# A two-layer gated decoder trunk on one core: output product in turns, later rope and attention, one more pair of banks

## The chip, the cores and the metric

One Trainium2 chip, one of its cores. The metric is device microseconds for one execution of the whole program, lower is better. The kernel before has a median of 1640.81 us over three runs (1640.46 to 1642.13).

## The reference, cut to what matters

Everything is float32. There are 256 tokens of width 1024, and two layers. Each layer adds five results to the residual stream `x` in turn:

```
x = x + 0.5 * swiglu(rms_norm(x, ffn1_norm), ffn1_w_gu, ffn1_w_down)
h = rms_norm(x, mix_norm);  z = h @ w_in            # q, k, v, HGRN inputs, gates
y_a = dilated_attention(rope(q), rope(k), v) @ w_att_branch   # 4 heads, 3 dilations each
y_b = (rms_norm(hgrn2(...)) * silu(og)) @ w_hgrn_branch       # 8 heads
x = x + (sigmoid(gate_a) * y_a + sigmoid(gate_b) * y_b) @ w_mix_out
x = x + cross_attention(rms_norm(x, xattn_norm), rms_norm(mem, mem_norm), ...)  # 4 heads
x = x + 0.5 * swiglu(rms_norm(x, ffn2_norm), ffn2_w_gu, ffn2_w_down)
```

The result is a last `rms_norm(x, final_norm)`.

## The kernel before

Activations lie with features on the 128 partitions and the 256 tokens along the free axis. A product is computed in blocks of 128x128 weights. Each float32 operand is split in a high and a low part, and three partial products are kept. For one block TensorE runs two matmuls in `fm`: the high weights against both parts of the activation at once (L323, 512 columns) and the low weights against the high part (L324, 256 columns).

**The weight stream.** Weights arrive from memory in the order of use, 16 blocks a transfer, issued by SyncE. `Stream.prep` splits them in *halves* of 8 blocks: ScalarE casts the high parts (tile `whi`, L104), VectorE subtracts for the low parts (tile `wlo`, L110). When the first block of half i is taken, `take` emits the high cast of half i+3 and the low subtraction of half i+2, and then calls `tick`. So the order of the instructions on each engine is the order in which this Python program emits them, and a low part that is emitted behind other VectorE work waits for that work.

**Ticks.** Each tick (one per half) runs the functions whose count set by `defer(n, ...)` has come down to zero, and then one step of one side generator (`side(generator, period)`). Rope, attention, the HGRN recurrence and the norm of the memory are such side work; they stand between the halves of the large products.

**Accumulators.** The large products accumulate in `pair` tiles: two PSUM banks each, a pool of three. Small products use `bank` tiles: one PSUM bank each, a pool of two. An fm product of two output blocks fills one pair in 16 weight blocks (two halves). `fm_beside` fills two pairs, block by block in turns, and hands over both at the end; before the change only the first FFN of the first layer uses it (L336, L337). `add_halves` copies one half of a pair (L344, ScalarE) and adds the other one tick later (L347, VectorE), which frees the pair.

**Places that the change and the prediction speak of.**

- *Memory norm.* `mem_stats` runs as side work in the first FFN of the first layer. `Norm.steps` sums with TensorE (L395), computes the reciprocal root with VectorE and GpSimd (L398, L401), scales an identity matrix (L404) and, two steps later, spreads the result with a matmul (L408).
- *Rope and attention.* `query_key` has an evacuation, `stage1` (L878 to L880: ScalarE copies and a GpSimd product), then one tick later `stage2` (L884, L885 on VectorE), and one tick after that, for the last of a head's three dilations, `attention` begins as side work with period 2. Attention's first step does the scores (L739 in a bank, L743 in a pair) and emits the softmax (L748 to L754); its second step normalises (L756 to L758), an empty step follows, then come the transposes (L765 to L770) and the value product (L777, L779).
- *HGRN.* `hgrn` holds a pair from its output matmuls (L692, L694) until L705, some four ticks later, once for each half of the heads.
- *Mixer output.* After the merged branch products (att and hgrn, whose last results are put in operand form by L277 and L280), `mm_resid` forms `w_mix_out` in four fm products of two blocks each. Each hands its pair to `Resid.take`: two additions into x (L434), then for two blocks of x the next operand (L287 on ScalarE, L288 on VectorE) and the squares for the next norm (L374 on ScalarE, L376 on VectorE).
- *Cross attention.* After the last value product (L988, L989 take it out) four heads form their output in one bank each (L293 to L295), and `o.put` takes each out (L277, L280).
- *The end.* `Last.finish` sums the squares over the partitions: L477 on what was accumulated so far, L478 on the last block's squares (L454).

Of the kernel before, what the change touches and what calls it, by code (L numbers as in the profile page):

```python
# [127 lines left out]
def build(tc, a, nchunks):  # L128
# [25 lines left out]
    def bank():  # L154
        return psum1.tile([P, 512], F32, name="bank")
# [15 lines left out]
    def defer(n, fn):  # L171
        deferred.append([n, fn])
# [193 lines left out]
    class Norm:  # L366
# [25 lines left out]
        def steps(self, keep=None):  # L392
            st = bank()
            for i in range(2):
                nc.tensor.matmul(st[:, i:i + 1], self.acc[:, i * P:(i + 1) * P], ones[:, :1],  # L395
                                 start=True, stop=True)
            ms = tiny.tile([P, 2], F32, name="ms")
            nc.vector.tensor_scalar(ms, st[:, :2], 1.0 / D, EPS, op0=OP.mult, op1=OP.add)  # L398
            pool = tiny if keep is None else consts
            self.r = pool.tile([P, 2], F32, name="rstd" + (keep or ""))  # L400
            nc.gpsimd.tensor_tensor(self.r, ms, mhalf[:, :2], op=OP.pow)  # L401
            dg = tmp()
            for i in range(2):
                nc.vector.tensor_scalar(dg[:, i * P:(i + 1) * P], ident, self.r[:, i:i + 1], None, op0=OP.mult)  # L404
            yield
            yield
            b = bank()
            nc.tensor.matmul(b[:, :T], ones, dg, start=True, stop=True)  # L408
            self.bc = (tiny if keep is None else consts).tile([P, T], F32, name="bc" + (keep or ""))
            nc.scalar.copy(self.bc, b[:, :T])  # L410
# [29 lines left out]
    class Last:  # L440
# [32 lines left out]
        def finish(self, g):  # L473
            st = pair()
            for i in range(2):
                s = slice(i * P, (i + 1) * P)
                nc.tensor.matmul(st[:, i:i + 1], self.acc[:, s], ones[:, :1], start=True, stop=False)  # L477
                nc.tensor.matmul(st[:, i:i + 1], self.sq[:, s], ones[:, :1], start=False, stop=True)  # L478
            ms = tiny.tile([P, 2], F32, name="ms")
            r = tiny.tile([P, 2], F32, name="rstd")  # L480
            nc.vector.tensor_scalar(ms, st[:, :2], 1.0 / D, EPS, op0=OP.mult, op1=OP.add)
            nc.gpsimd.tensor_tensor(r, ms, mhalf[:, :2], op=OP.pow)
            self.turn(KD - 1, g)
            for i in range(2):
                o, y = self.o[i], a["y"][i * P:(i + 1) * P]
                nc.vector.tensor_scalar(o[:, :512], o[:, :512], r[:, i:i + 1], None, op0=OP.mult)
                nc.scalar.activation(o[:, 512:], self.b[i], AF.Copy, scale=r[:, i:i + 1])
                nc.sync.dma_start(y[:, :512], o[:, :512])
                (nc.sync, nc.scalar)[i].dma_start(y[:, 512:], o[:, 512:])

    def mm_resid(name, l, act, K, res):
        n = 2 if K == KD else 1
        for j in range(0, KD, n):
            fm([(name, l, (j + i) * P, act, K) for i in range(n)],
               lambda left, right, j=j: res.take(j, left, right))

# [238 lines left out]
    def attention(l, h, qk, v, out):  # L735
        b0, b1 = bank(), pair()
        for g in range(NG):
            q, k = qk[g]
            nc.tensor.matmul(b0[:, g * P:(g + 1) * P], q[:, :P], k[:, :P], start=True, stop=True)  # L739
        for g in range(NG):  # L740
            q, k = qk[g]
            d = b1[:, g * T:(g + 1) * T]
            nc.tensor.matmul(d, q[:, P:], k, start=True, stop=True)  # L743
        s0, s1 = slot(), slot()
        sc = float(P) ** -0.5
        mx = tiny.tile([P, 2], F32, name="mx")
        den = tiny.tile([P, 2], F32, name="den")
        nc.vector.scalar_tensor_tensor(s0[:, :384], b0[:, :384], sc, cst[:, C_M0:C_M0 + 384], op0=OP.mult, op1=OP.add)  # L748
        nc.vector.scalar_tensor_tensor(s1[:, :768], b1[:, :768], sc, cst[:, C_M1:C_M1 + 768], op0=OP.mult, op1=OP.add)
        nc.vector.tensor_reduce(mx[:, 0:1], s0[:, :384], axis=AX.X, op=OP.max)  # L750
        nc.vector.tensor_reduce(mx[:, 1:2], s1[:, :768], axis=AX.X, op=OP.max)
        nc.vector.tensor_scalar(mx, mx, -1.0, None, op0=OP.mult)
        nc.scalar.activation(s0[:, :384], s0[:, :384], AF.Exp, bias=mx[:, 0:1], accum_out=den[:, 0:1])
        nc.scalar.activation(s1[:, :768], s1[:, :768], AF.Exp, bias=mx[:, 1:2], accum_out=den[:, 1:2])  # L754
        yield
        nc.vector.reciprocal(den, den)  # L756
        nc.vector.tensor_scalar(s0[:, :384], s0[:, :384], den[:, 0:1], None, op0=OP.mult)
        nc.vector.tensor_scalar(s1[:, :768], s1[:, :768], den[:, 1:2], None, op0=OP.mult)  # L758
        yield
        yield  # L760
        b0, b1 = bank(), pair()
        p0, p1 = slot(), slot()
        for g in range(NG):
            d = b1[:, g * T:(g + 1) * T]
            nc.tensor.transpose(d[:, :P], s0[:, g * P:(g + 1) * P], ident)  # L765
            nc.tensor.transpose(d[:, P:], s1[:, g * T:g * T + P], ident)
        for g in range(NG):
            nc.tensor.transpose(b0[:, g * P:(g + 1) * P], s1[:, g * T + P:(g + 1) * T], ident)
        nc.scalar.copy(p0[:, :768], b1[:, :768])
        nc.scalar.copy(p1[:, :384], b0[:, :384])  # L770
        yield
        while ("v", l) not in flags:
            yield True
        b = bank()
        hs = slice(h * P, (h + 1) * P)
        for g in range(NG):
            nc.tensor.matmul(b[:, :T], v(g, 0)[:, hs], p0[:, g * T:(g + 1) * T], start=g == 0, stop=False)  # L777
        for g in range(NG):
            nc.tensor.matmul(b[:, P:T], v(g, 1)[:, hs], p1[:, g * P:(g + 1) * P], start=False, stop=g == NG - 1)  # L779
        out.put(h, b[:, :T])  # L780
        yield
# [8 lines left out]
    def mixer(l, res, nxt):  # L790
# [76 lines left out]
        def query_key(u):  # L867
# [5 lines left out]
            def evac(left, right):  # L873
# [3 lines left out]
                def stage1():  # L877
                    nc.scalar.copy(r[:64], d[64:])  # L878
                    nc.scalar.copy(r[64:], d[:64])  # L879
                    nc.gpsimd.tensor_tensor(r, r, both(sb), op=OP.mult)  # L880
                    defer(1, stage2)

                def stage2():
                    nc.vector.tensor_tensor(d, d, both(cb), op=OP.mult)  # L884
                    nc.vector.tensor_tensor(d, d, r, op=OP.add)  # L885
                    if g == NG - 1:
                        qk = [(row(2 * i), row(2 * i + 1)) for i in range(NG)]
                        defer(1, lambda: side(attention(l, hd, qk, v, aout), 2))
                add_halves(d, left, right, stage1)
            c = g * 512 + hd * P  # L890
            fm([("w_in", l, CQ + c, h, KD), ("w_in", l, CK + c, h, KD)], evac)
# [29 lines left out]
                add_halves(two(t), left, right, stage1, last)  # L921
            fm([("w_att_branch", l, j * P, aout, AH), ("w_hgrn_branch", l, j * P, hout, HH)], evac)
        r = nxt()
        mm_resid("w_mix_out", l, mg, KD, r)
        return r


# [33 lines left out]
    def xattn(l, res, hm, nxt):  # L961
# [30 lines left out]
        drain()  # L992
        o = Act()
        for hd in range(XH):
            b = bank()
            for d in range(2):
                o0 = (2 * (hd % 2) + d) * P
                for c in range(2):
# [114 lines left out]
```

## Time and profile before

| | |
|---|---|
| median of three runs | 1640.81 us |
| the profiled execution's own time | 1640.77 us |
| its span in the profile | 1639.0 us |
| TensorE busy | 1618.5 us, 99% of the span |
| VectorE busy | 1240.8 us, 76% |
| ScalarE busy | 925.7 us, 56% |
| DMA | mean 176 GB/s |
| granted TensorE clock, mean | 0.998 |

The span runs from the program's first instruction to its last; the profiled execution took 1.8 us more than it. Times in the views are counted from the start of the span. PE is TensorE, PEld its weight loads, DVE VectorE, ACT ScalarE, POOL GpSimd, SP SyncE. Since two matmuls overlap, the end of a matmul in the trace is a model; the distance between the starts of matmuls is the safer measure.

### The profile page before, as it was taken

The numbers are of one execution on the slowest core, as the hardware profiler recorded it, in microseconds if no ns is written. First come the engines' busy times: TensorE is split into PE (matmuls) and PEld (weight loads), VectorE is DVE, ScalarE is ACT, GpSimd is POOL, SyncE is SP. The second block draws the span as 40 slices with busy tenths as digits, with TensorE's granted clock in tenths as the row PEclk, the third lists the DMA queues.
The fourth block names the chain that finished last, engine by engine and source line by source line (L and its number), as shares of the span: only waits on it lengthen the run. The fifth ranks groups of instructions, "written<-read, shape, count | busy, mean of one in ns | idle before, by whom it ended". The sixth has DMA issues, their size and how long they took to land.

```text
span 1639.0 us, 26419 instructions
## 1 busy us (share of the span) xinstructions
PE 1618.5 (99%) x10818; PEld 1414.8 (86%) x10818; DVE 1240.8 (76%) x1804; ACT 925.7 (56%) x1381; POOL 63.0 (4%) x46
## 2 busy tenths in 40 slices
PE   9999999999999999999999999999999999999998
PEld 7888888888888888888888888888888888888887
DVE  7887687767868868877677776777788787688764
ACT  6665454656565656655456655546565656466542
POOL 0000000102100000000000000001111000000000
PEclk9999999999999999999999999999999999999999
DMA  8555554434445534555555564544334454355552
GB/s 303 183 181 211 199 182 180 155 130 154 154 154 180 197 137 171 190 190 196 184 185 197 182 223 176 191 172 150 144 133 159 174 180 179 129 206 180 193 191 79
DMA packets 41593, 288.94 MB, mean 176 GB/s; under 512 B 4864, under 2 KB 4992, under 8 KB 7424
## 3 DMA queue, kind: packets, MB, share of 16 engines
q1 hardware_dynamic: 41040, 286.67, 49.0%
q8 instruction: 85, 1.39, 0.3%
q10 hardware_dynamic: 432, 0.59, 0.1%
q14 instruction: 36, 0.29, 0.1%
HBM read 286.18 MB, written 1.05 MB: 175 GB/s over the span
## 4 chain that ended last, share of the span: by engine, by line
PE 90%; DVE 6%; ACT 2%; issue 1%; DMA 0%; POOLq 0%; POOL 0%; ACTq 0%; DVEq 0%
PE pair L323 49%; PE pair L324 25%; PE pair L297 3%; PE pair L298 3%; PE pair L299 3%; DVE wlo L110 2%; PE bank L645 1%; DVE join L347 1%; DVE slot L280 1%; PE bank L777 1%; PE pair L336 1%; DVE join L917 1%; PE pair L743 0%; PE bank L293 0%; PE bank L294 0%
## 5 line engine op out<-in xcount | busy, mean ns | idle before, releaser
L323 PE MATMUL pair<-slot,whi 128*128 128x512 f32 x3808 | 1337.4, 395 | 4.8 <-DVE slot L280 2.5
L324 PE MATMUL pair<-slot,wlo 128*128 128x256 f32 x3808 | 1065.9, 280 | 0.0
L323 PEld LDWEIGHTS pair<-slot,whi 128*128 128x128 f32 x3808 | 713.4, 187 | 167.4 <-DVE slot L347 3.1
L324 PEld LDWEIGHTS pair<-slot,wlo 128*128 128x128 f32 x3808 | 719.2, 189 | 0.6
L110 DVE TENSOR_TENSOR wlo<-raw,whi 128x1024 fp32r<-128x1024 f32 x532 | 640.1, 1221 | 43.2 <-ACT whi L104 42.9
L104 ACT CAST whi<-raw 128x1024 fp32r<-128x1024 f32 x532 | 546.7, 1046 | 15.5 <-PE pair L299 6.1
L344 ACT COPY join<-pair 128x512 f32<-128x512 f32 x136 | 79.6, 586 | 181.8 <-PE pair L324 181.7
L347 DVE TENSOR_TENSOR join<-pair,join 128x512 f32<-128x512 f32 x136 | 93.7, 690 | 107.1 <-ACT join L344 107.0
L287 ACT ACTIVATE slot<-x,vecs 128x256 fp32r<-128x256 f32 x64 | 30.9, 506 | 133.2 <-DVE x L434 132.0
L297 PE MATMUL pair<-whi,slot 128*128 128x512 f32 x224 | 89.2, 398 | 0.0
L299 PE MATMUL pair<-whi,slot 128*128 128x512 f32 x224 | 87.4, 390 | 0.0
L298 PE MATMUL pair<-wlo,slot 128*128 128x512 f32 x224 | 87.4, 390 | 0.0
L344 ACT COPY slot<-pair 128x512 f32<-128x512 f32 x48 | 28.1, 586 | 102.7 <-PE pair L324 102.7
L277 ACT CAST slot<-join 128x256 fp32r<-128x256 f32 (+1 forms) x120 | 51.7, 435 | 50.8 <-DVE join L919 26.0
L434 DVE SCALAR_TENSOR_TENSOR x<-pair,x 128x256 f32<-128x256 f32 (+1 forms) x80 | 42.5, 531 | 49.2 <-PE pair L324 47.7
L511 ACT ACTIVATE tmp<-join 128x256 f32<-128x256 f32 x88 | 36.4, 417 | 52.5 <-DVE join L510 52.4
L510 DVE TENSOR_TENSOR join<-join,bc 128x512 f32<-128x512 f32 x88 | 60.5, 692 | 5.1 <-ACT bc L410 2.4
L880 POOL TENSOR_TENSOR join<-join,sinb 128x512 f32<-128x512 f32 x24 | 42.1, 1753 | 421.7 <-ACT join L879 392.8
L280 DVE TENSOR_TENSOR slot<-join,slot 128x256 fp32r<-128x256 f32 (+1 forms) x120 | 54.0, 455 | 2.8 <-ACT slot L277 2.8
L347 DVE TENSOR_TENSOR slot<-pair,slot 128x512 f32<-128x512 f32 x48 | 33.1, 689 | 27.5 <-ACT slot L344 27.4
L288 DVE SCALAR_TENSOR_TENSOR slot<-x,vecs,slot 128x256 fp32r<-128x256 f32 x64 | 29.6, 484 | 27.0 <-ACT slot L287 27.0
L299 PEld LDWEIGHTS pair<-whi,slot 128*128 128x128 f32 x224 | 42.0, 188 | 9.0
(184 smaller groups left out, 1029.9 us busy)
## 6 DMA issues: line engine op xcount, KB each, us to landing
raw<-w SPq DMA_DIRECT2D x266, 1024.0 KB, 4.8
slot<-mem SPq DMA_DIRECT2D x6, 512.0 KB, 6.7
raw<-w SPq DMA_DIRECT2D x3, 512.0 KB, 7.8
y<-slot SPq DMA_DIRECT2D x3, 256.0 KB, 2.3
cst<-cst SPq DMA_DIRECT2D x1, 721.0 KB, 10.2
x<-x SPq DMA_DIRECT2D x2, 256.0 KB, 4.3
x<-x SPq DMA_DIRECT2D x1, 512.0 KB, 7.0
raw<-w ACTq DMA_DIRECT2D x1, 256.0 KB, 5.1
```

What stands on the lines that cost most here:

```text
L104: nc.scalar.copy(self.hi[i], r)
L110: nc.vector.tensor_tensor(self.lo[i], r, self.hi[i].bitcast(F32), op=OP.subtract)
L277: nc.scalar.copy(h, src)
L280: nc.vector.tensor_tensor(l, src, h.bitcast(F32), op=OP.subtract)
L297: nc.tensor.matmul(out, ah, wh, start=first, stop=False)
L298: nc.tensor.matmul(out, ah, wl, start=False, stop=False)
L299: nc.tensor.matmul(out, al, wh, start=False, stop=last)
L323: nc.tensor.matmul(whole[:, i * 512:(i + 1) * 512], wh, act.parts(k), start=k == 0, stop=False)
L324: nc.tensor.matmul(whole[:, i * 512:i * 512 + T], wl, act.hi(k), start=False, stop=k == K - 1)
L344: nc.scalar.copy(d, right)
L347: nc.vector.tensor_tensor(d, left, d, op=OP.add)
L510: nc.vector.tensor_tensor(two(t), two(t), both(n.bc), op=OP.mult)
```

## The change

Six edits, which together move work but add or drop no arithmetic:

1. `Norm.steps(keep=...)`, the norm of the memory, yields once more before its last matmul.
2. `Last.finish` issues both sums over the earlier squares, then both over the last ones, and each token block's sum gets a bank of its own.
3. `mm_resid` can form its first four output blocks with `fm_beside`, two pairs by turns; the mixer's output product does so.
4. `stage2` of rope comes two ticks after `stage1` instead of one, and attention starts two ticks after the last `stage2` instead of one.
5. Attention loses the empty step between the normalisation and the transposes.
6. In cross attention the output of heads 2 and 3 goes to half a pair each in place of a bank.

```diff
@@ Norm.steps
             yield
             yield
+            if keep:
+                yield
             b = bank()
@@ Last.finish
             for i in range(2):
-                s = slice(i * P, (i + 1) * P)
-                nc.tensor.matmul(st[:, i:i + 1], self.acc[:, s], ones[:, :1], start=True, stop=False)
-                nc.tensor.matmul(st[:, i:i + 1], self.sq[:, s], ones[:, :1], start=False, stop=True)
+                nc.tensor.matmul(st[:, i * 512:i * 512 + 1], self.acc[:, i * P:(i + 1) * P], ones[:, :1],
+                                 start=True, stop=False)
+            for i in range(2):
+                nc.tensor.matmul(st[:, i * 512:i * 512 + 1], self.sq[:, i * P:(i + 1) * P], ones[:, :1],
+                                 start=False, stop=True)
...
-            nc.vector.tensor_scalar(ms, st[:, :2], 1.0 / D, EPS, op0=OP.mult, op1=OP.add)
+            nc.vector.tensor_scalar(ms, two(st)[:, :, 0], 1.0 / D, EPS, op0=OP.mult, op1=OP.add)
@@ mm_resid
-    def mm_resid(name, l, act, K, res):
+    def mm_resid(name, l, act, K, res, turns=False):
         n = 2 if K == KD else 1
-        for j in range(0, KD, n):
+        first = 0
+        if turns:
+            first = 4
+            fm_beside([(name, l, j * P, act, K) for j in range(4)],
+                      [lambda left, right, j=j: res.take(j, left, right) for j in (0, 2)])
+        for j in range(first, KD, n):
@@ attention, between the normalisation and the transposes
         yield
-        yield
@@ query_key
-                    defer(1, stage2)
+                    defer(2, stage2)
...
-                        defer(1, lambda: side(attention(l, hd, qk, v, aout), 2))
+                        defer(2, lambda: side(attention(l, hd, qk, v, aout), 2))
@@ mixer
-        mm_resid("w_mix_out", l, mg, KD, r)
+        mm_resid("w_mix_out", l, mg, KD, r, True)
@@ xattn
-            b = bank()
+            b = bank() if hd < 2 else pair()[:, :512]
```

In the lists below line numbers of the changed kernel are 2 to 9 higher than before; the names of the tiles tell which instruction is which.

**The mixer's output product, VectorE, from the last operand of the branch products on.** L110 are low parts of weight halves, L434 (before) and L436 (changed) open an evacuation of `Resid.take`, L288 and L376 belong to it. Before:

```order
L280 TENSOR_TENSOR slot<-join,slot 128x256
L110 TENSOR_TENSOR wlo<-raw,whi 128x1024
L280 TENSOR_TENSOR slot<-join,slot 128x256
L110 TENSOR_TENSOR wlo<-raw,whi 128x1024
L434 SCALAR_TENSOR_TENSOR x<-pair,x 128x512 x2
L288 SCALAR_TENSOR_TENSOR slot<-x,vecs,slot 128x256 x2
L376 TENSOR_TENSOR tmp<-tmp 128x256
L110 TENSOR_TENSOR wlo<-raw,whi 128x1024 x2
L434 SCALAR_TENSOR_TENSOR x<-pair,x 128x512 x2
L288 SCALAR_TENSOR_TENSOR slot<-x,vecs,slot 128x256 x2
L376 TENSOR_TENSOR tmp<-tmp 128x256 x2
L110 TENSOR_TENSOR wlo<-raw,whi 128x1024 x2
```

With the change:

```order
L280 TENSOR_TENSOR slot<-join,slot 128x256
L110 TENSOR_TENSOR wlo<-raw,whi 128x1024
L280 TENSOR_TENSOR slot<-join,slot 128x256
L110 TENSOR_TENSOR wlo<-raw,whi 128x1024 x3
L436 SCALAR_TENSOR_TENSOR x<-pair,x 128x512 x2
L288 SCALAR_TENSOR_TENSOR slot<-x,vecs,slot 128x256 x2
L376 TENSOR_TENSOR tmp<-tmp 128x256
L436 SCALAR_TENSOR_TENSOR x<-pair,x 128x512 x2
L288 SCALAR_TENSOR_TENSOR slot<-x,vecs,slot 128x256 x2
L376 TENSOR_TENSOR tmp<-tmp 128x256 x2
L110 TENSOR_TENSOR wlo<-raw,whi 128x1024 x2
```

The two low parts that stood between the first two evacuations now stand ahead of both, and the first two evacuations stand back to back ahead of the next low part.

**The third attention head and the second HGRN output, VectorE.** L748 to L752 take the head's scores, L705 (before) and L714 (changed) read the pair that HGRN holds, L347 frees the pair of a large product. Before:

```order
L347 TENSOR_TENSOR slot<-pair,slot 128x512
L854 TENSOR_TENSOR slot<-slot,bc 128x512
L748 SCALAR_TENSOR_TENSOR slot<-bank,cst 128x384
L749 SCALAR_TENSOR_TENSOR slot<-pair,cst 128x768
L750 TENSOR_REDUCE mx<-slot 128x1
L751 TENSOR_REDUCE mx<-slot 128x1
L752 TENSOR_SCALAR mx<-mx 128x2
L110 TENSOR_TENSOR wlo<-raw,whi 128x1024 x2
L347 TENSOR_TENSOR slot<-pair,slot 128x512
L705 TENSOR_TENSOR slot<-pair,rs 128x512 x2
```

With the change (there L757 to L761 are the head's scores):

```order
L347 TENSOR_TENSOR slot<-pair,slot 128x512
L714 TENSOR_TENSOR slot<-pair,rs 128x512 x2
L110 TENSOR_TENSOR wlo<-raw,whi 128x1024
L757 SCALAR_TENSOR_TENSOR slot<-bank,cst 128x384
L758 SCALAR_TENSOR_TENSOR slot<-pair,cst 128x768
L759 TENSOR_REDUCE mx<-slot 128x1
L760 TENSOR_REDUCE mx<-slot 128x1
L761 TENSOR_SCALAR mx<-mx 128x2
```

The head's scores are now taken after HGRN's pair has been read, where before they were taken while HGRN still held it.

## Rows read from the trace of the kernel before

**Rows 1.** The page's first part (busy time) and its chain, by engine.
```profile
PE 1618.5 (99%) x10818; PEld 1414.8 (86%) x10818; DVE 1240.8 (76%) x1804; ACT 925.7 (56%) x1381; POOL 63.0 (4%) x46
...
PE 90%; DVE 6%; ACT 2%; issue 1%; DMA 0%; POOLq 0%; POOL 0%; ACTq 0%; DVEq 0%
```

**Rows 2.** The waits: who for whom, us in total, times, longest.
```profile
PE pair L323 <- DVE slot L280: 2.5, 2, 1.6
...
PE pair L323 <- DVE slot L347: 2.3, 2, 1.2
...
PE bank L293 <- DVE slot L280: 1.6, 2, 0.8
...
PE bank L739 <- DVE slot L885: 1.5, 2, 0.8
...
PE pair L478 <- ACT tmp L454: 1.3, 1, 1.3
...
PE bank L408 <- DVE tmp L404: 1.0, 1, 1.0
```

**Rows 3.** Timeline of PE, second layer, mixer output: start, us, what, [idle before].
```profile
1319.73 0.27 PE L324 MATMUL pair<-slot,wlo 128*128 128x256 f32 x1
1321.61 0.47 PE L323 MATMUL pair<-slot,whi 128*128 128x512 f32 x1 [1.61 <-DVE slot L280]
```

**Rows 4.** Timeline of PE, first layer, scores of the third head.
```profile
406.45 1.46 PE L743 MATMUL pair<-slot 128*128 128x256 f32 x6
409.08 0.50 PE L323 MATMUL pair<-slot,whi 128*128 128x512 f32 x1 [1.17 <-DVE slot L347]
```

**Rows 5.** Timeline of DVE at the same place, and HGRN's last read there.
```profile
408.34 0.69 DVE L347 TENSOR_TENSOR slot<-pair,slot 128x512 f32<-128x512 f32 x1
...
416.99 1.28 DVE L705 TENSOR_TENSOR slot<-pair,rs 128x512 f32<-128x512 f32 x2
```

**Rows 6.** Timeline of DVE, first layer, rope of the first head.
```profile
304.29 0.69 DVE L885 TENSOR_TENSOR slot<-slot,join 128x512 f32<-128x512 f32 x1
```

**Rows 7.** Timeline of DVE, cross attention, last value evacuation.
```profile
609.18 0.75 DVE L989 SCALAR_TENSOR_TENSOR slot<-pair,rstdmem,slot 128x512 fp32r<-128x512 f32 x1 [0.76 <-ACT slot L988]
```

**Rows 8.** Timeline of PE at the end.
```profile
1631.87 0.36 PE L477 MATMUL pair<-cst,tmp 128*128 128x1 f32 x2
1632.09 0.36 PE L478 MATMUL pair<-cst,tmp 128*128 128x1 f32 x2
```

**Rows 9.** Timeline of DVE, first layer, mixer output.
```profile
512.83 0.42 DVE L280 TENSOR_TENSOR slot<-join,slot 128x256 fp32r<-128x256 f32 x1
513.16 1.22 DVE L110 TENSOR_TENSOR wlo<-raw,whi 128x1024 fp32r<-128x1024 f32 x1
515.08 1.42 DVE L434 SCALAR_TENSOR_TENSOR x<-pair,x 128x512 f32<-128x512 f32 x2 [0.69 <-PE pair L324]
...
518.43 2.35 DVE L110 TENSOR_TENSOR wlo<-raw,whi 128x1024 fp32r<-128x1024 f32 x2
520.73 1.42 DVE L434 SCALAR_TENSOR_TENSOR x<-pair,x 128x512 f32<-128x512 f32 x2
...
524.39 2.35 DVE L110 TENSOR_TENSOR wlo<-raw,whi 128x1024 fp32r<-128x1024 f32 x2
```

**Rows 10.** Timeline of PE there, around the end of its first product.
```profile
514.53 0.40 PE L323 MATMUL pair<-slot,whi 128*128 128x512 f32 x1
514.76 0.28 PE L324 MATMUL pair<-slot,wlo 128*128 128x256 f32 x1
514.88 0.40 PE L323 MATMUL pair<-slot,whi 128*128 128x512 f32 x1
```

**Rows 11.** L323 in the branch products, first and second layer: min/median/max ns, first, last start.
```profile
L323 PE MATMUL pair<-slot,whi x80: 395/398/403, 475.9 to 503.8; 128*128 128x512 f32 x80
...
L323 PE MATMUL pair<-slot,whi x82: 392/394/395, 1283.8 to 1311.9; 128*128 128x512 f32 x82
```

**Rows 12.** Busy time by window, the product in turns of the first FFN.
```profile
13.00:21.00 8.00, 8.00 (x48) 7.00 (x47) 6.90 (x11) 6.30 (x9) 0.00 (x0) 1.00 1.03 410
```

## The prediction

> **What bounds the kernel now.** I read the page's first part and its chain first: TensorE is busy for 99% of the span and holds 90% of the chain [rows 1]. So only time in which TensorE stands still, or runs slower, counts. The list of waits then says where it stands still after the start: behind L280, L347, L885 and L404, nine waits in all, 2.5 + 2.3 + 1.6 + 1.5 + 1.0 = 8.9 us, and 1.3 us at the end [rows 2]. The timeline shows what one costs. From an L324 to the next L323 is 0.12 us normally [rows 10], but 1.88 us at the longest wait: 1.76 lost where the list has 1.61 [rows 3]. The list leaves out the modelled tail of the matmul before, so I add 0.2 us for each of the nine places. Nowhere does the list of waits show a large product waiting for a low part of the weights once the start is past: the low parts are always in time. That matters below.
>
> One block takes 0.35 us (514.53 to 514.88) [rows 10], a half of 8 blocks 2.8 us.
>
> **The change, part by part.** No arithmetic is added or dropped and no DMA moves; SyncE's order is the same.
>
> *Memory norm.* The one matmul L408 waits 1.0 us for L404 [rows 2]. One tick later is 2.8 us later, more than the wait. Saved: 1.0 + 0.2 = 1.2.
>
> *Rope and attention, the first head.* In each layer L739 waits for rope's L885, 1.5 us in both [rows 2]; L885 ends at 304.98 [rows 6]. Its stage moves one tick on VectorE and the scores two, so the scores gain a net tick, 2.8 us. Saved: 1.5 + 2 x 0.2 = 1.9. The softmax has less time to the transposes, since those stay where they were among the blocks: the scores come two ticks later and the empty step, two ticks, is gone. What is left is four ticks, 11 us.
>
> *Rope and attention, the third head.* After the scores L743 the next large product waits until 409.08 [rows 4]; L347 ends at 409.03 [rows 5]. It waits for a pair: one is held by HGRN until L705 at 418.3 [rows 5], one holds the scores, and the third is that of the product just before. In the changed order HGRN's pair is read before the third head's scores are taken, so a pair is free. Saved in two layers: 2.3 + 0.4 = 2.7. The second head now falls inside the first such hold. There its scores come in the middle of a product, and 8 more blocks, 2.8 us, pass before another pair is wanted. VectorE has only to read the scores in that time (0.55 + 0.95 us of L748 and L749, were it free), so I cost this at nothing; what hides it is those 8 blocks. If VectorE is behind by more than a microsecond the cover is gone, and that is a rival.
>
> *Cross attention.* The first matmul of head 2 waits for L280 to read head 0's bank, 1.6 us in two layers [rows 2]. With a pair of its own it needs only the values. The last part of these is ready when L989 ends at 609.93 [rows 7], about when it is wanted: tight, but not late by more than 0.1. The next product begins a microsecond earlier, and its first operands are those of head 0, ready by then. Saved: 1.6 + 0.4 = 2.0.
>
> *The end.* After L454 the tail had L478, L477, L478; now the L477 of the second block is done before. One step, 1631.87 to 1632.09 [rows 8]: 0.2. The wait of 1.3 stays.
>
> *Mixer output, what goes.* In each layer the product reaches the operands of block 6 before L280 (ends 513.25 [rows 9]) has made their low part, 2.5 us together [rows 2]. With four output blocks in turns, block 6 comes after 24 weight blocks instead of 12, which is 4.2 us more. Saved: 2.5 + 0.4 = 2.9.
>
> *Mixer output, what comes.* This is the one part that I expect to cost. An evacuation takes VectorE 3.35 us for the first (515.08 to 518.43) and 3.66 for the later ones (520.73 to 524.39) [rows 9]. They came 16 blocks apart, with two low parts (2.35 us) between. Now two are emitted back to back, and the low part of the half after next stands behind both. Let T be the start of the block after the product in turns. Pair one is complete two blocks before T, and an evacuation starts 0.2 us after the next block's start (514.88 to 515.08 [rows 9, 10]), so VectorE starts at T - 0.5, ends both at T + 6.5, and the low part (1.22 us [rows 9]) at T + 7.7. TensorE wants it after 16 blocks and one L323 (0.23 us), at T + 5.8. It stands for 1.9 us, say 2.0 with the handing over. VectorE is then late for the rest of the stage: next low part T + 8.9, third evacuation T + 12.6, next low part T + 13.8, wanted at T + 13.4. Another 0.3 to 0.4. The fourth comes right. Sum 2.3 a layer, 4.6 in two. Bounds: nothing, if VectorE finds the time to do the low parts first, which its fixed order excludes for the first of them; and 3.4 a layer, if the evacuation begins only when both pairs are complete (0.7 later) and the lag is paid twice more. I take 2.3, from the rows of the very instructions. ScalarE's casts run one half further ahead and are not late. The other pairs are free: the product in turns takes two that the branch products freed, and the next takes the third.
>
> **Sum.** Gone: 1.2 + 1.9 + 2.7 + 2.0 + 0.2 + 2.9 = 10.9. Come: 4.6. Net 6.3 us, against the profiled execution's own time of 1640.77 (span 1639.0 and 1.8 around it; the median is 1640.81): **1634.5 us**.
>
> One thing I can't place. The same blocks run at two paces: L323 starts 0.353 us apart in the first layer (27.9 us for 79 steps) and 0.347 in the second (28.1 for 81) [rows 11], with nothing waiting. The pace seems to be picked where small matmuls interrupt. The change moves such places among some 700 blocks of the two mixers; if half of them change pace that is 350 x 0.006 = 2 us either way. It goes into the range.
>
> **The rivals.**
>
> *The burst costs nothing* (the low parts are in time after all). For it: they have always been in time, and VectorE is busy for only 76% [rows 1]. Against it: the order, and the arithmetic above. Time: 1634.5 - 4.6 = 1629.9.
>
> *New waits for a pair at the second head*, in place of those at the third. For it: that head now lies inside HGRN's hold, with a product, HGRN and scores on three pairs. Against it: the 8 blocks of cover. It decides if VectorE reads the scores more than 2.8 us after they are done. Price up to what the third head paid, 2.7: 1637.2.
>
> *The burst at its upper bound*, 3.4 a layer: 1634.5 + 2.2 = 1636.7.
>
> *The wait on rope only moves.* The change would not do what it says if L885 went back as far as the scores. The orders speak against it (one tick against two). Price 1.9: 1636.4.
>
> *Slower: four banks in turns cost the clock.* In the product in turns TensorE writes a different bank at each block. If that made it fall to the lower of its two levels, 1.2 in place of 2.4 GHz, a block of 0.35 us would take up to 0.35 more, for 32 blocks in each layer: 22 us, so 1657. It decides if the engine stops between blocks for the change of bank. The first FFN already has such a product: 48 matmuls, 24 blocks, in 8.00 us at a granted clock of 1.00, full level [rows 12], a pace as good as anywhere. The Trainium skill (TensorE: Matmul & The Clock Gate, section "A second HAM failure mode: psum-queue depth-cycling") tells of a kernel that cycled through PSUM banks at each iteration, idled briefly between groups and lost throughput to the clock's changes. By that rule this edit would lose the 22 us; the row says that four banks in turns did not do it here.
>
> **How the numbers follow.** What a measurement of this kernel can tell from no change is about 0.2%, 3.3 us: below 1637.5 is faster, above 1644.1 slower. Chances: my forecast 0.60; the burst free 0.10; new pair waits 0.13; the burst at its bound 0.08; rope only moved 0.05; the clock 0.02; the remaining 0.02 for a delay that I haven't seen. With 2 us of pace about half of the pair-wait case and a third of the next two land within 0.2%, and so does a tail of the forecast, where two of the small costs come together. So faster 0.78, within 0.2% 0.18, slower 0.04. The range reaches down to a free burst and up past the pair waits with the pace against me: 1630.5 to 1638.5.
>
> **What would show it.** Right: in the list of waits of the changed kernel TensorE no longer waits for L885, L404, or L347 after scores, nor L280 in the mixer's output and in cross attention; in their place it waits for a low part (L110) of about 2.0 us in each layer's output product, 16 blocks after the product in turns, and a little more 16 blocks later. VectorE shows two evacuations without a low part between, 7.0 us long. Wrong: no wait on L110 there (the burst is free), a wait on L749's successor or L347 after the second head's scores (pair), or blocks of the product in turns further apart than 0.36 us (clock). A total above 1638.5 without any of these waits would mean that the paces decide more than I think.

## The result, and the profile after

The changed kernel takes 1633.01 us in the median of 4 runs (1631.77 to 1633.60), against 1640.65 us for the kernel before, run beside it (1640.46 to 1642.13). The ratio is 0.9950 with a 95% interval of 0.9938 to 0.9963: 0.5% faster, clear of the 0.2% that the forecast counted as no change. Forecast were 1634.5 us and a range of 1630.5 to 1638.5. The profiled execution took 1632.85 us, with a span of 1631.0.

The first part and the chain of the changed kernel's page, against [rows 1]:

```profile
PE 1616.2 (99%) x10818; PEld 1413.6 (87%) x10818; DVE 1241.0 (76%) x1804; ACT 925.1 (57%) x1381; POOL 64.0 (4%) x46
...
PE 98%; DVE 1%; ACT 0%; DMA 0%; issue 0%; POOLq 0%; ACTq 0%; DVEq 0%
```

The busy shares have hardly moved. The chain has: VectorE held 6% of it before and holds 1% now. The list of waits says why. Of the changed kernel, TensorE after the start:

```profile
PE pair L324 <- DVE wlo L110: 3.5, 2, 1.7
...
PE pair L481 <- ACT tmp L456: 1.1, 1, 1.1
```

All of L280, L347, L885 and L404 of [rows 2] are gone, in both products and both layers. One new wait has come, for a low part of the weights, once in each layer, and the one at the end is 0.2 us shorter. The new wait stands where the forecast put it. PE's timeline of the changed kernel, first layer: the first block after the product in turns, the sixteenth after that, and the one eight blocks later.

```profile
514.09 0.40 PE L323 MATMUL pair<-slot,whi 128*128 128x512 f32 x1
...
519.75 0.39 PE L323 MATMUL pair<-slot,whi 128*128 128x512 f32 x1
521.88 0.39 PE L324 MATMUL pair<-slot,wlo 128*128 128x256 f32 x1 [1.73 <-DVE wlo L110]
...
526.62 0.39 PE L323 MATMUL pair<-slot,whi 128*128 128x512 f32 x1
...
527.31 0.39 PE L323 MATMUL pair<-slot,whi 128*128 128x512 f32 x1
527.81 0.39 PE L324 MATMUL pair<-slot,wlo 128*128 128x256 f32 x1
```

From 519.75 to 521.88 are 2.12 us, before rounding, where 0.23 is normal: 1.89 lost. From 527.31 to 527.81 another 0.26 goes. And the cause, in the DVE timeline of the same place, against [rows 9]:

```profile
513.60 1.42 DVE L436 SCALAR_TENSOR_TENSOR x<-pair,x 128x512 f32<-128x512 f32 x2 [2.24 <-PE pair L337]
...
516.95 1.41 DVE L436 SCALAR_TENSOR_TENSOR x<-pair,x 128x512 f32<-128x512 f32 x2
518.93 0.89 DVE L288 SCALAR_TENSOR_TENSOR slot<-x,vecs,slot 128x256 fp32r<-128x256 f32 x2 [0.58 <-ACT slot L287]
519.74 0.95 DVE L376 TENSOR_TENSOR tmp<-tmp 128x256 f32<-128x256 f32 x2
520.60 2.35 DVE L110 TENSOR_TENSOR wlo<-raw,whi 128x1024 fp32r<-128x1024 f32 x2
```

Two evacuations in one piece, 513.60 to 520.60, and the low part only behind them. VectorE was idle for 2.24 us just before; that matters for the experiments.

The first L395 (the sum of a norm) of each norm cuts the program into stages that can be compared. Each number is the distance between two such starts (or the start or end of the span), worked out from both traces:

| stage, up to the sum of | before, us | changed, us | gain | forecast |
|---|---|---|---|---|
| first norm | 23.66 | 22.72 | 0.94 | 0 |
| the memory | 75.77 | 75.77 | 0 | 0 |
| first mixer's norm | 102.06 | 100.88 | 1.18 | 1.2 |
| first cross attention's norm | 336.00 | 333.87 | 2.13 | 1.45 |
| the FFN's norm after it | 104.34 | 103.38 | 0.96 | 1.0 |
| second mixer's norm (two stages) | 368.05 | 368.05 | 0 | 0 |
| second cross attention's norm | 335.49 | 334.05 | 1.44 | 1.45 |
| the FFN's norm after it | 104.44 | 103.38 | 1.06 | 1.0 |
| end of the span | 189.17 | 188.94 | 0.23 | 0.2 |
| sum | 1638.98 | 1631.04 | 7.94 | 6.3 |

### The profile page after: what moved, and what is told of

The parts are those of the page before. It is cut to its first block, busy times and chain, and to the rows that moved or that the text cites. A ratio compares the mean times of both kernels' runs of the same rounds, so it can differ in the third digit from the quotient of the medians.

```text
span 1631.0 us, 26415 instructions
## 1 busy us (share of the span) xinstructions
PE 1616.2 (99%) x10818; PEld 1413.6 (87%) x10818; DVE 1241.0 (76%) x1804; ACT 925.1 (57%) x1381; POOL 64.0 (4%) x46
## 3 DMA queue, kind: packets, MB, share of 16 engines
HBM read 286.18 MB, written 1.05 MB: 176 GB/s over the span
## 4 chain that ended last, share of the span: by engine, by line
PE 98%; DVE 1%; ACT 0%; DMA 0%; issue 0%; POOLq 0%; ACTq 0%; DVEq 0%
PE pair L323 52%; PE pair L324 27%; PE pair L297 3%; PE pair L299 3%; PE pair L298 3%; PE pair L336 1%; PE bank L654 1%; PE pair L337 1%; PE pair L752 1%; PE bank L785 1%; PE pair L701 0%; DVE x L436 0%; PE bank L295 0%; PE bank L294 0%; PE bank L293 0%; PE bank L787 0%
## 5 line engine op out<-in xcount | busy, mean ns | idle before, releaser
L323 PE MATMUL pair<-slot,whi 128*128 128x512 f32 x3744 | 1315.4, 395 | 0.0
L324 PE MATMUL pair<-slot,wlo 128*128 128x256 f32 x3744 | 1048.0, 280 | 3.6 <-DVE wlo L110 3.5
L323 PEld LDWEIGHTS pair<-slot,whi 128*128 128x128 f32 x3744 | 701.5, 187 | 158.4 <-DVE slot L280 0.4
L324 PEld LDWEIGHTS pair<-slot,wlo 128*128 128x128 f32 x3744 | 707.0, 189 | 5.5 <-DVE wlo L110 4.8
L110 DVE TENSOR_TENSOR wlo<-raw,whi 128x1024 fp32r<-128x1024 f32 x532 | 641.8, 1225 | 37.3 <-ACT whi L104 36.8
L347 DVE TENSOR_TENSOR join<-pair,join 128x512 f32<-128x512 f32 x136 | 93.8, 690 | 105.1 <-ACT join L344 105.0
L436 DVE SCALAR_TENSOR_TENSOR x<-pair,x 128x256 f32<-128x256 f32 (+1 forms) x80 | 42.5, 531 | 52.3 <-PE pair L324 46.3
L280 DVE TENSOR_TENSOR slot<-join,slot 128x256 fp32r<-128x256 f32 (+1 forms) x120 | 54.0, 455 | 2.8 <-ACT slot L277 2.8
L347 DVE TENSOR_TENSOR slot<-pair,slot 128x512 f32<-128x512 f32 x48 | 33.1, 689 | 30.0 <-ACT slot L344 29.7
L288 DVE SCALAR_TENSOR_TENSOR slot<-x,vecs,slot 128x256 fp32r<-128x256 f32 x64 | 29.6, 484 | 27.4 <-ACT slot L287 27.4
```

The source lines that it names most:

```text
L110: nc.vector.tensor_tensor(self.lo[i], r, self.hi[i].bitcast(F32), op=OP.subtract)
L280: nc.vector.tensor_tensor(l, src, h.bitcast(F32), op=OP.subtract)
L323: nc.tensor.matmul(whole[:, i * 512:(i + 1) * 512], wh, act.parts(k), start=k == 0, stop=False)
L324: nc.tensor.matmul(whole[:, i * 512:i * 512 + T], wl, act.hi(k), start=False, stop=k == K - 1)
L347: nc.vector.tensor_tensor(d, left, d, op=OP.add)
```

## The experiments

Each ran beside the kernel before (medians 1640.65 to 1640.76 in the three sets). Edits 1, 2 and 6 were not taken back by themselves; what is said of them rests on the waits and the stages above.

### Edit 3 taken back: no_turns

```diff
-        mm_resid("w_mix_out", l, mg, KD, r, True)
+        mm_resid("w_mix_out", l, mg, KD, r)
```

> The changed kernel with the product in turns undone (edit 3 alone taken back; the other five edits stay). Theory, burst: edit 3 loses more than it saves. The two waits on low parts per layer (1.89 + 0.26 and 1.89 + 0.18 us of TensorE's standing, 4.2 together) go, and the waits for L280 that edit 3 removed (1.07 and 1.76 us, 2.8 together) come back: 1.4 us faster than the changed kernel, about 1631.6. Rival, edit 3 pays for itself: the low parts would be late in the old order too, now that the heads have moved, and only the 2.8 us come back: about 1635.8. With either the pace of the blocks can shift the time by 0.7 us a layer.

Measured: 1630.72 us (5 runs, 1629.45 to 1631.42), ratio to before 0.9937 (0.9925 to 0.9949). That is 2.3 us faster than the changed kernel. Its waits:

```profile
PE pair L323 <- DVE slot L280: 1.8, 2, 0.9
```

The waits on L110 are gone and the one on L280 is back, 1.05 us between starts in each layer (the second was 1.76 before). So 4.2 go, 2.1 come. The part of the change that the title names first costs time; the other five edits bring more than the whole.

### Edit 3 alone: turns_alone

The kernel before, with the diff's part on `mm_resid` and its call.

> The kernel before with edit 3 alone, the product in turns. Theory, burst: about 4.2 us of waits on low parts come and 2.8 us of waits for L280 go, so 1.4 us slower than the kernel before, about 1642.1; the waits for L885, L347 after the third head, L404 and L293 all stay as in the kernel before. Rival, edit 3 pays for itself: as fast as the kernel before or up to 2.8 us faster, 1637.8 to 1640.6.

Measured: 1642.99 us (11 runs, 1639.58 to 1644.58), ratio 1.0011 (1.0002 to 1.0019). 2.3 us slower than before, where 1.4 were expected, and its runs lie far apart. The waits are as expected: L110 for 3.5 us, and L347, L293, L404 and rope as in [rows 2]. The profiled execution is the slowest of the eleven (1644.58 us). In it the two mixer stages lost 0.89 and 1.28 us against the kernel before, 2.2 together. What was not expected lies in the stage of the memory's norm, which took 103.84 us, 1.78 more than in the kernel before, at the same wait on L404, ahead of anything that edit 3 touches. L323 from that wait to the next norm, in the kernel before (min/median/max of one, first and last start):

```profile
L323 PE MATMUL pair<-slot,whi x273: 391/391/586, 107.0 to 201.9; 128*128 128x512 f32 x137
```

in edit 3 alone:

```profile
L323 PE MATMUL pair<-slot,whi x273: 395/398/580, 106.7 to 203.4; 128*128 128x512 f32 x137
```

272 steps in 94.9 us and in 96.7. The same blocks at two paces in two executions. This is the term that the forecast could not place, and a run below takes it up. The medians leave about 0.9 us over the expected 1.4, and no trace places it. Four of the eleven runs have a mean granted clock of 0.997, where none of the seventeen of the kernel before, run beside it, has less than 0.998; that the clock fell behind a stop in them is possible, but not shown.

### The evacuations spread: spread

```diff
-                      [lambda left, right, j=j: res.take(j, left, right) for j in (0, 2)])
+                      [lambda left, right, j=j: (defer(2, lambda: res.take(j, left, right)) if j
+                                                 else res.take(j, left, right)) for j in (0, 2)])
...
-               lambda left, right, j=j: res.take(j, left, right))
+               lambda left, right, j=j: defer(2, lambda: res.take(j, left, right)) if turns else res.take(j, left, right))
...
-        mn = memn["n"]
+        mn, n.wait = memn["n"], 4
```

> The changed kernel, with the second, third and fourth evacuation of the mixer's output two ticks later (and the next norm two ticks later, since it needs their squares), so that two low parts stand between any two evacuations on VectorE. Theory, burst: only the order of VectorE's work makes TensorE wait, not its amount. Both waits on L110 go and none takes their place: 4.2 us faster than the changed kernel, about 1628.8; no wait for L376, L395 or L347 beyond 0.5 us. Rival, amount: VectorE is full in this stage, so the low parts come late further on, or the pairs are held too long and TensorE waits for L436: at most 1 us is gained, 1632 or more.

Measured: 1628.62 us (5 runs, 1627.92 to 1629.26), ratio 0.9925 (0.9913 to 0.9937), 4.4 us faster than the changed kernel. This is all that TensorE waits for in it, the start included:

```profile
PE bank L1032 <- ACT warm L1029: 3.2, 1, 3.2
PE pair L481 <- ACT tmp L456: 1.1, 1, 1.1
PE pair L336 <- ACT whi L74: 0.8, 1, 0.8
```

VectorE does the same work in the stage. Its order alone made TensorE wait. Of the versions run three cannot be told apart and are the fastest: this one, low_first_late_norm and pace_probe below (medians 1628.62, 1628.98 and 1628.39 us).

### One low part ahead of the burst: low_first and low_first_late_norm

```diff
-                      [lambda left, right, j=j: res.take(j, left, right) for j in (0, 2)])
+                      [lambda left, right, j=j: (j or W.prep(0, W.n_lo), res.take(j, left, right)) for j in (0, 2)])
...
-               lambda left, right, j=j: res.take(j, left, right))
+               lambda left, right, j=j: (turns and W.prep(0, W.n_lo), res.take(j, left, right)))
```

> The changed kernel, with one low part more emitted ahead of the burst, the third and the fourth evacuation of the mixer's output, in the 2.2 us in which VectorE idles before the burst; the evacuations stay where they are. Theory, burst: the waits on L110 go (by the durations of this stage the next low part is ready 0.9 us before it is wanted, the one after the third evacuation 0.4 before): 4.2 us faster, about 1628.8, as with the evacuations spread. Rival, amount: the waits only move by one half and shrink by less than half: 1631 or more.

Measured: 1635.23 us (6 runs, 1632.17 to 1638.34), ratio 0.9965 (0.9953 to 0.9977). Neither theory had what came: the waits on L110 are gone, and the kernel is 2.2 us slower than the changed one. In its place, low_first's PE timeline:

```profile
531.55 0.28 PE L324 MATMUL pair<-slot,wlo 128*128 128x256 f32 x1
533.79 1.01 PE L395 MATMUL bank<-cst,tmp 128*128 128x1 f32 x4 [1.97 <-DVE tmp L376]
534.67 0.77 PE L323 MATMUL pair<-slot,whi 128*128 128x512 f32 x1
...
535.45 0.63 PE L323 MATMUL pair<-slot,whi 128*128 128x512 f32 x1
...
536.09 0.63 PE L323 MATMUL pair<-slot,whi 128*128 128x512 f32 x1
```

The next norm's sum waits for the last squares, which the low parts moved ahead have delayed. And then the blocks are 0.64 us apart. Windows of low_first (stretch, its length and PE's busy time, PEclk, DMA share, GB/s):

```profile
533.00:536.00 3.00, 2.21 (x8) 0.63 0.03 8
536.00:539.00 3.00, 3.00 (x11) 0.50 0.87 311
539.00:542.00 3.00, 3.00 (x14) 0.73 0.56 194
```

and of the changed kernel around its own stop:

```profile
519.00:523.00 4.00, 2.27 (x13) 1.00 0.00 0
523.00:527.00 4.00, 4.00 (x25) 1.00 0.67 250
```

After the stop of 1.97 us the granted clock went to 0.50, the lower level of 1.2 GHz; after the changed kernel's 1.73 it stayed at 1.00, that of 2.4 GHz. The stage that begins there took 106.54 us in the first layer against 103.39 in the changed kernel: beside the stop of 2.1 us between starts, 3.15 us of slower blocks behind it. In the second layer, behind a stop of nearly the same length, it was 1.66 us (105.04 against 103.38), and the trace's record of the clock has 0.50 for 3.4 us there where it has 6.8 us in the first. This profiled execution is one of the two slowest of six (1638.33 us, mean granted clock 0.996); the fastest took 1632.17 at 0.998, so not every execution pays that much.

The remedy is one tick more before the norm (`n.wait = 3` in `xattn`):

> The kernel low_first with the next norm one tick later. Theory: what low_first lost stands in one place, the norm's first matmul L395, which waited 2.1 us for the last squares L376 in each layer, after which the granted clock stood at half for some 6 us; one tick is 2.8 us and takes both away. No wait on L110 or L376, granted clock 1.00 in the stretch after: 1628.8, as the kernel spread (1628.62). Rival: VectorE's amount of work in the stage is the limit and the wait moves on to the next low part or to the next L395: 1632 or more.

Measured: 1628.98 us (5 runs, 1626.09 to 1629.87), ratio 0.9927 (0.9914 to 0.9941): as fast as spread. No wait but those of the start and the end is left. So low_first had lost time in that one place, and a second order of the same work on VectorE is as good as the first.

### A longer stop: longer_stop

```diff
-                      [lambda left, right, j=j: res.take(j, left, right) for j in (0, 2)])
+                      [lambda left, right, j=j: (j and nc.vector.tensor_tensor(slot(), xall[:, :1024],
+                          xall[:, :1024], op=OP.add), res.take(j, left, right)) for j in (0, 2)])
```

> The changed kernel with an idle VectorE addition of 128x1024 (about 1.2 us, its result is read by nobody) between the first two evacuations of the mixer's output, so that TensorE's wait on the low part grows from 1.9 to about 3.1 us, and the later ones with it. In the kernel low_first a wait of 2.1 us ahead of four small matmuls was followed by some 6 us at half the granted clock; in the changed kernel 1.9 us ahead of large ones was not. Theory, the length of the stop: after the longer stop the granted clock falls to 0.50 here too, and each layer loses 1.2 to 1.5 us of wait and some 2 to 3 of clock: 1639 to 1642. Rival, what follows the stop: large matmuls follow, the clock stays at 1.00, and only the wait is paid, 1.2 to 1.5 a layer: 1635.4 to 1636.

Measured: 1638.66 us (10 runs, 1636.26 to 1640.82), ratio 0.9989 (0.9979 to 0.9998). PE's timeline:

```profile
518.82 0.40 PE L323 MATMUL pair<-slot,whi 128*128 128x512 f32 x1
522.28 0.58 PE L324 MATMUL pair<-slot,wlo 128*128 128x256 f32 x1 [3.06 <-DVE wlo L110]
```

and its windows:

```profile
521.00:525.00 4.00, 2.72 (x8) 0.57 0.13 20
525.00:529.00 4.00, 4.00 (x15) 0.57 0.58 242
529.00:533.00 4.00, 4.00 (x25) 1.00 0.60 231
```

Large matmuls follow this stop, and the clock falls all the same, in both layers (the second is not shown here: 0.50 from 1331 to 1335). So the small matmuls in low_first were not needed for it. The stage took 337.64 us, 3.77 more than in the changed kernel, of which the waits account for 1.1 (3.22 between starts against 1.89 + 0.26). The Trainium skill (TensorE: Matmul & The Clock Gate, section "HAM oscillation — how this bites in real kernels") tells of a matmul kernel whose clock is throttled at each wait for data; low_first's and this trace agree that a wait can be followed by a fall (1.97 and 3.06 us), and the changed kernel's wait of 1.73 us, without a fall, shows that here not every one is. The runs' times lie 4.6 us apart. The mean granted clock of each run goes with them: 0.994 and 0.995 in the three slowest, 0.997 in the other seven, 0.998 in all runs of the changed kernel. By these figures the clock fell in every execution, and in most of them for less time than in the profiled one (0.995). So the median lies just under the theory's 1639, and well above the rival's 1636.

### Edits 4 and 5: heads_back, empty_step, stage2_early

heads_back undoes both edits:

```diff
-                    defer(2, stage2)
+                    defer(1, stage2)
...
-                        defer(2, lambda: side(attention(l, hd, qk, v, aout), 2))
+                        defer(1, lambda: side(attention(l, hd, qk, v, aout), 2))
...
         yield
+        yield
         b0, b1 = bank(), pair()
```

> The changed kernel with edits 4 and 5 taken back (rope and attention as before, the rest as changed). Theory, the forecast's terms: TensorE waits again for rope (0.92 us of excess distance between starts, twice) and behind the third head's scores (1.52, twice): 4.9 us slower than the changed kernel, about 1637.9. Rival, the earlier waits only shifted other waits ahead: with the mixer's output in turns part of them is absorbed, 1634 to 1636.

Measured: 1638.65 us (11 runs, 1636.39 to 1639.82), ratio 0.9986 (0.9978 to 0.9995); 5.6 us slower than the changed kernel. Both waits are back with the sizes of [rows 2]:

```profile
PE pair L323 <- DVE slot L347: 2.3, 2, 1.2
PE bank L748 <- DVE slot L894: 1.5, 2, 0.8
```

Part of the rest over the expected 4.9 has a place too. The stop at the low part is 1.84 us here, in both layers. In the first the clock stayed at 1.00; in the second, windows of heads_back from the end of the stop:

```profile
1332.00:1334.00 2.00, 2.00 (x7) 0.53 0.03 8
1334.00:1336.00 2.00, 2.00 (x9) 0.62 0.91 283
1336.00:1338.00 2.00, 2.00 (x13) 1.00 0.58 242
```

The same stop, in one execution, once with a fall of the clock behind it and once without.

empty_step puts back only the `yield`:

> The changed kernel with edit 5 alone taken back (the empty step between normalisation and transposes stands again, so the transposes and the value product come two ticks later). Theory: edit 5 was free and saved nothing by itself; no new wait over 0.3 us, within 1 us of the changed kernel (1632 to 1634), the pace of the blocks deciding within that. Rival: the last head's value product now comes too close to the branch products, and TensorE waits for its operand once a layer: 1 to 3 us slower, 1634 to 1636.

Measured: 1634.04 us (5 runs, 1632.78 to 1635.62), ratio 0.9959 (0.9946 to 0.9971).

```profile
PE bank L786 <- ACT slot L778: 1.1, 2, 0.6
```

The last head's value product (L786) stands directly behind its transposes, without large blocks between, and waits for ScalarE's copy, 0.59 us between starts in each layer; the two mixers take 0.69 and 0.64 us longer. That is the rival's mechanism, at the low end of its 1 to 3 us, and the theory's "no new wait over 0.3 us" is refuted. The medians, 1.0 us apart with runs that overlap, would not show it by themselves. heads_back, with neither edit, has no such wait. So edit 5 pays for what edit 4 would cost at the last head, where the side work is drained.

stage2_early undoes the first line of heads_back alone:

> The changed kernel with the first half of edit 4 taken back: rope's second stage one tick after the first, as before; attention still starts two ticks after it, so the scores come one tick earlier than in the changed kernel and one later than before. Theory: the wait on rope stays away (the scores alone needed the tick), but the third head's scores come back into HGRN's hold of a pair and its wait returns in both layers: 1.5 us each, about 1636. Rival: one tick is enough for both, no wait on L347 over 0.3 us: 1632 to 1634.

Measured: 1637.99 us (10 runs, 1636.41 to 1639.15), ratio 0.9984 (0.9974 to 0.9993), 5.0 us slower than the changed kernel. The total is nearer to the theory's, the places are others:

```profile
PE pair L773 <- DVE slot L347: 1.6, 2, 0.8
PE pair L752 <- DVE slot L347: 0.5, 2, 0.3
PE pair L774 <- DVE slot L767: 0.4, 2, 0.2
PE pair L773 <- DVE slot L766: 0.3, 1, 0.3
```

The wait on rope stays away, and scores (L752) wait 0.3 us at most, where the theory had 1.5. But it is now the transposes (L773) of the heads that meet a pair still held, or come before VectorE has normalised (L766, L767). A tick earlier shifts all steps of a head against the pairs, not the scores alone. The waits between starts sum to 1.6 and 2.1 us; the mixers took 2.3 and 2.4 more.

### What sets the pace: pace_probe

Spread, with an idle matmul ahead of two products in each layer:

```diff
+        n == 2 and nc.tensor.matmul(bank()[:, :T], ones, cst[:, :T], start=True, stop=True)
```

> The kernel spread with one idle float32 matmul of 256 columns (its result is read by nobody) ahead of the first block of the mixer's output product and of cross attention's output product. In the traces so far a run of blocks that follows such a matmul without a wait goes at 0.347 us a block, and other runs at 0.347 or 0.353. Theory, the matmul ahead sets the pace: the 80 blocks of cross attention's output product, 0.3533 in every trace so far, go at 0.347 in both layers, 0.5 us less each, against about 0.35 us for the matmul: in all within 1 us of spread. Rival, the pace belongs to the place (its operands or banks): it stays at 0.353, and the probes cost 1.4 us.

Measured: 1628.39 us (4 runs, 1627.63 to 1628.85), ratio 0.9924 (0.9910 to 0.9937), the same as spread. L323 of the second layer's cross attention output, in spread:

```profile
L323 PE MATMUL pair<-slot,whi x64: 395/398/403, 1408.7 to 1431.0; 128*128 128x512 f32 x64
```

in pace_probe:

```profile
L323 PE MATMUL pair<-slot,whi x64: 392/395/579, 1409.9 to 1432.0; 128*128 128x512 f32 x64
```

63 steps in 22.3 us and in 22.1, the latter with a first block that takes 0.53 instead of 0.35; so 62 steps at 0.347 where all traces without the probe have 0.353. Operands and place are the same. Here the matmul ahead changed the pace, and the run of blocks kept it until the next interruption. That what stands ahead always decides is not shown: the second layer's branch products have the same matmuls ahead in spread and in the changed kernel, and went at 0.347 in the one and 0.353 in the other. What the matmul does to the blocks behind it was not found. The gain, 0.4 us a layer, about equals the probe's price.

## Why the prediction was right

*The bound, and the list of waits as the measure.* Right. All nine waits went, most at the sizes of the list plus 0.2 us each: 1.18 against 1.2 for the memory's norm, 0.96 and 1.06 against 1.0 for cross attention, 1.84 against 1.9 for rope. Behind the third head's scores the list and 0.2 us were too little: 1.52 us each between starts, 3.0 together against 2.7. heads_back brings back these and the waits on rope, no_turns those of the mixer's output.

*The memory's norm can be worth more than its wait.* Only two traces have that wait, and behind it the 272 blocks went at the faster pace in one and at the slower in the other. With edit 1 they follow L410 without a stop, and this stage took 100.88 us in nine traces and 100.73 in the tenth. The forecast priced the stop alone.

*The burst.* Right in its place, mechanism and size. The forecast counted from T, the first block after the product in turns, which is 514.09: VectorE was to start at T - 0.5, end both evacuations at T + 6.5 and the low part at T + 7.7, with TensorE wanting it at T + 5.8. The rows give 513.60, 520.60, 521.82 and 519.98, which is T - 0.49, + 6.51, + 7.73 and + 5.89. Forecast 2.3 us a layer; measured 1.89 + 0.26 = 2.15 and 1.89 + 0.18 = 2.07, which is a little under. That order alone is the cause is shown by two kernels which keep the turns and the work and lose the wait.

*The balance of edit 3.* The forecast had 2.9 saved and 4.6 lost. Measured are 2.8 saved against the kernel before, only 2.1 beside the other edits, and 4.2 lost. So the sign is right: a net loss, inside a change that gains.

*The rivals.* The free burst is refuted by the waits on L110. The burst at its upper bound, 3.4 a layer, was not reached. Pair waits at the second head did not come: no L347 after scores in the list. stage2_early shows how near they were, one tick away. The wait on rope did not move elsewhere: TensorE waits nowhere for its second stage (L893) in the list. The rule on banks in turns did not bite: the blocks of the product in turns (502.8 to 514.0) stood at a granted clock of 1.00, 0.353 us apart.

*What was off: the sum was 1.6 us short of the gain between the two profiled executions (7.94 us).* 0.94 lies in the first stage, which the change does not touch: that part of the gain is chance. TensorE's first blocks lie 0.64 us apart and later 0.35, and the switch comes at another time in each execution. Windows of the kernel before:

```profile
8.00:10.00 2.00, 2.00 (x8) 1.00 1.02 418
10.00:12.00 2.00, 2.00 (x8) 1.00 1.06 440
```

of the changed one:

```profile
8.00:10.00 2.00, 2.00 (x8) 1.00 1.04 385
10.00:12.00 2.00, 2.00 (x12) 1.00 1.05 432
```

and of no_turns:

```profile
8.00:10.00 2.00, 2.00 (x13) 1.00 1.03 420
10.00:12.00 2.00, 2.00 (x13) 1.00 1.07 440
```

8 matmuls in 2 us, or 13. The view gives 1.00 for all of them, but it does so too where the trace holds no record of the clock. The first record, of 1.00, starts at 12.57 us in the kernel before, at 10.59 in the changed one and at 6.14 in no_turns, ahead of its first block. In the nine of the twelve traces that have such blocks, the last of them begins 0.4 to 1.0 us before that record; in the other three the record starts before the first block. And 0.64 is the distance that low_first showed at 0.50. So the first blocks went as at the lower level until the full clock was granted. The stage took 21.5 to 21.8 us in those three traces and 22.7 to 24.1 in the nine; why the clock is granted at another time in each execution stays open.

The other 0.67 is in the first mixer. There 3.51 us of waits (0.92, 1.52 and 1.07 between starts) went and 2.15 came, 1.36 net, but 2.13 were gained; in the second 4.20 went and 2.07 came, 2.13 net, and only 1.44 were gained. The rest, 0.8 one way and 0.7 the other, is the pace, for which the range had allowed 2 us. That the two nearly cancel is luck. The second layer's branch products are an example. 81 steps took 28.1 us before [rows 11], 0.347 each; now the 80 steps of

```profile
L323 PE MATMUL pair<-slot,whi x81: 395/398/403, 1275.7 to 1303.9; 128*128 128x512 f32 x81
```

take 28.2, 0.353 each.

## What to carry to other kernels

Where one engine issues its work in a fixed order, a product that finishes two results at once also delivers two evacuations at once; put the operands that the bound engine wants next ahead of them, or space them, and then look at who waits for the evacuations themselves, as the norm did here. Take a change of several edits apart: here one edit lost 2.3 us inside a change that gained 7.6, and repairing its order was worth more than taking it back. Price a stop of the bound engine by more than its length: what runs behind it may go at another pace or clock.

## What was not expected of the hardware

- A stop of TensorE of 1.97 us was followed by 6.8 us at a granted clock of 0.50, and one of 3.06 us as well; of two stops of 1.84 us in one execution the second was followed by 3.4 us of it and the first was not; those of 1.73 us in the changed kernel's profiled execution were not. The loss behind the stop in low_first, 3.15 us in the first layer and 1.66 in the second, was once larger and once smaller than the stop of 2.1 us between starts.
- The first blocks of the program lie 0.64 us apart until the trace's first record of the clock, which starts between 6.1 and 12.6 us in the twelve traces. It made 2.6 us between the shortest and the longest first stage.
- The same weight blocks, waiting for nothing, go at 0.347 or 0.353 us each at a granted clock of 1.00. After a stop either pace was seen at the same place; after a float32 matmul of 256 columns without a stop ahead it was 0.347 in these traces. Over the 272 blocks of one stage that made 1.8 us between the kernel before and turns_alone, which do the same up to there.
